# Two column vectors of a decoder layer: summed on the vector engine behind the head instead of on the tensor engine among the attention units

## The chip, the cores and the metric

One core of one Trainium2 chip. A kernel is timed in device microseconds from start to end of one launch; lower is better. Shown are the median, the lowest and the highest of three timed runs, and one further execution under the hardware profiler, whose trace is read here. The engines are TensorE (PE; its weight loads are PEld), VectorE (DVE), ScalarE (ACT), GpSimd (POOL) and SyncE (SP), which here issues nearly all DMAs. Each engine works through its own list of instructions in a fixed order.

## The reference, cut to what matters

One decoder layer on a sequence of 512 positions of width 1024, in float32. A conditioning vector c (1024) gives six vectors of 1024 by one matrix (1024 x 6144):

```python
mod = c @ w_ada[l] + b_ada[l]
sh1, sc1, gt1, sh2, sc2, gt2 = jnp.split(mod, 6, axis=-1)
h = rms_norm(x, g_pre_mix[l]) * (1.0 + sc1[:, None]) + sh1[:, None]
proj = h @ w_in[l]
...   # two attention groups: compressed/selected/window, and top-k sparse attention
x = x + gt1[:, None] * rms_norm(o, g_post_mix[l])
h = rms_norm(x, g_pre_ffn[l]) * (1.0 + sc2[:, None]) + sh2[:, None]
y = jnp.square(jax.nn.relu(h @ w_up[l])) @ w_down[l]
x = x + gt2[:, None] * rms_norm(y, g_post_ffn[l])
```

The change is about `sh2` and `sc2`, two of the six vectors: each a sum over 1024 rows of c times a row of 1024 numbers of `w_ada`, with a bias. They are needed when the second norm's output is made.

## The kernel before

Stages, in order of time: the head (0 to about 72 us: x is normed, transposed and multiplied with the first input weights, while sh1 and sc1 are summed); the projections (to about 145 us: chunks A, B, D, C, E of the input projection, rope, splitting of each float32 operand into a high and a low part, the indexer's scores); the attention units (to about 340 us: twelve units, with output projections between them); the second norm and the MLP (to the end). Products of split operands are three matmuls instead of one.

Order: steps are Python functions. `PLAN` (line 41) gives each group of steps a place t0 and a length dt; `place` (826) spreads the group's steps over numbered slots, and slot n is emitted with step n of the projection's pipeline (845 to 857, n from 0) or, from slot 19 on, with an attention unit (1083 to 1104). The framework then schedules all emitted instructions on a modelled time line: each engine's list is fixed before the run, and an instruction that comes later in the program can go ahead of one that is not ready in the model. `held` (592) makes a load come behind the loads of chunk D on SP's queue. `run` and `mix` (55 to 66) interleave lists evenly.

The six vectors: sh1 and sc1 in the head (`mod_sums`, 279). The gate gt1 is summed on TensorE by `vec_steps` (717) in group g1 = (17, 6). The gate gt2 is summed on DVE by `acc_steps` (672), with two loads and more ahead, beside the first MLP steps. The vectors sc2 (called a2) and sh2 go through `col_steps` (762), which uses `vec_steps`: eight loads of 512 KB each for a vector (two buffers with the tag vw, shared with gt1's loads), four matmuls for each load in four column groups of 32 (line 731), then for each half an ACT copy (767), four matmuls with a column of ones that turn the row into columns (770) and a DVE step with the bias (772). Groups a2 = (25, 2) and sh2 = (29, 3) put them among the attention units. Their results are used by `h2_steps` (1067, 1069).

Other names used: rw_C, rw_D, rw_E are raw weights of the chunks, uh and ul their high (ACT, 123) and low (DVE or POOL, 124) parts; pjB is B's projection, whose rope runs on POOL (`B1`, 478, and `rope`, 407); rwo_a and rwo_b are weights of the output projection; wk and m are the top-k rounds (574 to 579); mx is the row maximum of an attention unit (889). PSUM has four banks with the tag S, shared by projections, scores and these sums. The tag r (four buffers) is used from the MLP on (1141).

Of the kernel before, what the change touches and what calls it, by code (L numbers as in the profile page):

```python
# [9 lines left out]
F32 = mybir.dt.float32  # L10
# [3 lines left out]
OP = mybir.AluOpType  # L14
# [3 lines left out]
P = 128  # L18
T = 512
NT = 4  # L20
D = 1024
KT = 8
# [17 lines left out]

PLAN = dict(
    E=(19, 2.5), tk2=(17.8, 3.5), wa0=(25, 0.672), op00=(25.2, 0.48), wa1a=(25.1, 0.784), op10=(26.5, 0.462),
    wa1b=(25.73, 0.452), op01=(29.16, 0.2), op11=(27, 0.3), x20=(31.2, 0.1), x21=(27.3, 0.548), a2=(25, 2),
    sh2=(29, 3), wb0=(26.7, 0.49), wb1a=(28, 0.122), tk3=(21.5, 2.45), op20=(30.8, 0.48), wb1b=(30.5, 0.343),
    op21=(31.2, 0.96), op30=(32.5, 0.1), op31=(32.6, 0.49), h20=(32.2, 1.098), h21=(32.1, 0.549),
    x22=(32.6, 0.1), h22=(33.35, 1.68), x23=(33.6, 0.1), sD=(0, 0.48), cl=(0.2, 4.48), lC=(0.5, 0.1),
    sC=(3.7, 2.94), lE=(8.2, 0.1), sE=(8.3, 5.379), ix=(8.2, 5.88), cpe=(10, 0.1), ck1=(11.1, 1.077),
# [1 line left out]
    g1=(17, 6),  # L49
# [20 lines left out]
def layer_kernel(  # L70
# [7 lines left out]
    V, A, G, PE, SY = nc.vector, nc.scalar, nc.gpsimd, nc.tensor, nc.sync  # L78

    cst = ctx.enter_context(tc.tile_pool(name="cst", bufs=1))  # L80
    big = ctx.enter_context(tc.tile_pool(name="big", bufs=1))
# [23 lines left out]
    def m2(name, dt=F32):  # L105
        return big.tile([P, 512], dt, tag="m2", name=name, bufs=N_M)

    def st(shape, name):
        return sml.tile(shape, F32, tag="s%d" % int(np.prod(shape[1:])), name=name,
                        bufs=12 if shape[1] <= 8 else 2)  # L110

    def bank(tag, name, dt=F32):
        return psp.tile([P, 512], dt, tag=tag, name=name, bufs=4 if tag == "S" else 2)
# [16 lines left out]
    wa = w_ada[0].rearrange("(p k) n -> p k n", k=KT)  # L130
    wiv = w_in[0].rearrange("(k p) n -> p k n", p=P)
    xv = x[0].rearrange("(t p) d -> t p d", p=P)
    c_sb = cst.tile([P, KT], F32, name="c_sb")
# [48 lines left out]
    ones = cst.tile([P, P], F32, name="ones")  # L182
# [28 lines left out]
    colT = cst.tile([P, P], F32, name="colT")  # L211
# [122 lines left out]
    def behind(done, f, *args):  # L334

        with ExitStack() as es:
            for ins in done:
                es.enter_context(tc.issue_after(ins.ins))
            return f(*args)
# [203 lines left out]
    def Q2(nm, t):  # L543
        rv = heads(pjs[nm, t], 8)
        sks[nm, t] = [stack(rv[:, g * 4:g * 4 + 4, :], 4, f"{nm}{t}{g}", G) for g in range(2)]

    def Q3(nm, t):
        q = b4(f"q{nm}_{t}", F32R).rearrange("p (h q) -> p h q", q=P)
        for g in range(2):
            ps = stack_T(sks[nm, t][g], 4, f"{nm}{t}{g}")  # L550
            A.copy(q[:, g * 4:g * 4 + 4, :], ps.rearrange("p (h q) -> p h q", q=P))
        (qn if nm == "C" else qd)[t] = q
# [28 lines left out]
    def topk_steps(t):  # L581
        return [lambda: topk_round(t)] * 16 + [
            lambda: V.tensor_scalar(work[t], work[t], -3.2e38, NEG, op0=OP.is_gt, op1=OP.mult)]
# [8 lines left out]
    def held(f):  # L592

        return lambda: behind(d_loads[-1:], f)
# [122 lines left out]
    def vec_steps(c0, nm, finish):  # L717

        stt = {}

        def load(i):
            stt[i] = big.tile([P, 4, 256], F32, tag="vw", name=f"wv_{nm}{i}", bufs=2)
            n, q = divmod(i, 2)
            SY.dma_start(stt[i], wa[:, 4 * q:4 * q + 4, c0 + n * 256:c0 + n * 256 + 256])

        def mm(i):
            half, n, q = i // 4, i // 2 % 2, i % 2
            if i % 4 == 0:
                stt["ps"] = bank("S", f"vs_{nm}{half}")
            for j in range(4):  # L730
                PE.matmul(stt["ps"][32 * j:32 * j + 32, n * 256:n * 256 + 256],
                          c_sb[:, 4 * q + j:4 * q + j + 1].to_broadcast([P, 32]), stt[i][:, j, :],
                          start=(q == 0), stop=(q == 1))
            if i % 4 == 3:
                finish(half, stt["ps"])
        nv = 2
        seq = [lambda i=i: load(i) for i in range(nv)] + [none] * 6
        for i in range(8):
            seq.append(lambda i=i: mm(i))
            if i + nv < 8:  # L740
                seq.append(lambda i=i: load(i + nv))
        return seq
# [16 lines left out]
            V.tensor_tensor(g, pg, g, op=OP.mult)  # L759
        return [begin] + vec_steps(c0, "g1", finish)  # L760

    def col_steps(c0, nm):
        dst = cst.tile([P, KT], F32, name="col_" + nm)

        def finish(half, ps):
            acc = m2(f"acc_{nm}{half}")
            A.copy(acc, ps)
            pc = bank("S", f"cv_{nm}{half}")
            for k in range(4):
                PE.matmul(pc[:, k:k + 1], acc[:, k * P:(k + 1) * P], ones[:, 0:1], start=True, stop=True)  # L770
            h = half * 4
            V.scalar_tensor_tensor(dst[:, h:h + 4], pc[:, 0:4], 1.0 / 32.0,
                                   colT[:, c0 // P + h:c0 // P + h + 4], op0=OP.mult, op1=OP.add)
        return dst, vec_steps(c0, nm, finish)


    def w_in_chunk(c0, c1, nm, eng=V):
# [7 lines left out]
        def spl(i):  # L785
# [13 lines left out]
            lambda t, nm=nm: Q2(nm, t), lambda t, nm=nm: Q3(nm, t)), t) for t in range(NT) for nm in "C"]  # L799
    tl += tD + tC  # L800
    ix = [(t, h) for t in range(1, NT) for h in range(4)]
    tk = {t: topk_steps(t) for t in range(1, NT)}
    g1s = g1_steps(2 * D, g_post_mix)
    a2, a2s = col_steps(4 * D, "a2")
    sh2, sh2s = col_steps(3 * D, "sh2")
    a2s.append(lambda: V.scalar_tensor_tensor(a2, a2, 1.0, colT[:, 56:64], op0=OP.add, op1=OP.mult))
    el = []
    for t in range(NT + 2):
        if t < NT:
# [10 lines left out]
        ck1=[lambda: cmp_pack("k")], cv1=[lambda: cmp_pack("v")],  # L820
        ck2=[lambda: cmp_mm("k", 0), lambda: cmp_mm("k", 1)], cv2=[lambda: cmp_mm("v", 0), lambda: cmp_mm("v", 1)],
        ck3=[lambda: cmp_gelu("k"), lambda: cmp_out("k")], cv3=[lambda: cmp_gelu("v"), lambda: cmp_out("v")],
        tk1=tk[1], tk2=tk[2], tk3=tk[3], g1=[held(f) for f in g1s[:3]] + g1s[3:], a2=a2s, sh2=sh2s)
    slots = {n: [] for n in range(40)}

    def place(groups):
# [18 lines left out]
    for n in range(len(tl) + 3):  # L845
# [5 lines left out]
        while mm_done < min(want, len(mm_seq)):  # L851
            f, t = tl[mm_seq[mm_done]]
# [200 lines left out]
    def h2_steps(j):  # L1053
        def part(half):
# [8 lines left out]
            for i in range(4):  # L1063
# [14 lines left out]
               op11=outp_steps("a", 1, 1), x20=x2_steps(0), x21=x2_steps(1),  # L1078
               wb0=wout_steps("b", 0), wb1a=wb1[:2], op20=outp_steps("b", 2, 0), op30=outp_steps("b", 3, 0),
               wb1b=wb1[2:], op21=outp_steps("b", 2, 1), op31=outp_steps("b", 3, 1),  # L1080
               h20=h2_steps(0), h21=h2_steps(1), x22=x2_steps(2), x23=x2_steps(3), h22=h2_steps(2)))
    prev = None
    for n in range(16):
# [18 lines left out]
        if u is not None and u.nm == "w":  # L1102
            pc = cc
# [44 lines left out]
    def finish(t, half):  # L1148
        hs = [slice(i * 512, i * 512 + 512) for i in range(2)]
        jk = m2(f"fj_{t}{half}")  # L1150
        A.activation(jk, yacc[t][:, hs[half]], AF.Square, accum_out=sy[t][:, half:half + 1])
        (V if t == NT - 1 else G).tensor_tensor(yacc[t][:, hs[half]], yacc[t][:, hs[half]],
                                                res["g2"][:, hs[half]], op=OP.mult)
        if half == 1:
            rs = st([P, 1], "ro")
            rstd_of(rs, sy[t], V)
            for i in range(2):
                V.scalar_tensor_tensor(yacc[t][:, hs[i]], yacc[t][:, hs[i]], rs, x2[t][:, hs[i]],
                                         op0=OP.mult, op1=OP.add)
                SY.dma_start(ov[t][:, hs[i]], yacc[t][:, hs[i]])  # L1160
# [163 lines left out]
```

## Time and profile before

| | |
|---|---|
| timed runs | median 724.51 us (720.13 to 725.61) |
| profiled execution, own time | 724.97 us |
| its span, first to last instruction | 723.2 us |
| busy: PE / DVE / ACT / POOL | 674.7 / 510.3 / 373.9 / 191.9 us |
| mean granted clock of TensorE | 0.967 |

Busy times are of the whole span; stages differ, so the rows below are by stage. In a row of a timeline or a group stand line, engine, operation, output and inputs by the program's names (buffer numbers left out: vs_a2 is shown as vs_a), then shapes. In the chain of waits each piece is what released the next one, followed back from the last instruction.

### The profile page before, as it was taken

The numbers are of one execution on the slowest core, as the hardware profiler recorded it, in microseconds if no ns is written. First come the engines' busy times: TensorE is split into PE (matmuls) and PEld (weight loads), VectorE is DVE, ScalarE is ACT, GpSimd is POOL, SyncE is SP. The second block draws the span as 40 slices with busy tenths as digits, with TensorE's granted clock in tenths as the row PEclk, the third lists the DMA queues.
The fourth block names the chain that finished last, engine by engine and source line by source line (L and its number), as shares of the span: only waits on it lengthen the run. The fifth ranks groups of instructions, "written<-read, shape, count | busy, mean of one in ns | idle before, by whom it ended". The sixth has DMA issues, their size and how long they took to land.

```text
span 723.2 us, 10022 instructions
## 1 busy us (share of the span) xinstructions
PE 674.7 (93%) x3529; PEld 523.1 (72%) x3529; DVE 510.3 (71%) x1020; ACT 373.9 (52%) x755; POOL 191.9 (27%) x228
## 2 busy tenths in 40 slices
PE   3999989899998999799978999999999999999994
PEld 2678968777565676365668878888888888888883
DVE  5555458988997989775686539677597459695445
ACT  5343785435795669544464555433554355454221
POOL 3000285734523134222020022201140032231023
PEclk9899989999997999999999999999999999999998
DMA  9976630530316471462295212452144312322103
GB/s 293 311 232 188 199 88 1 117 116 30 118 30 191 133 171 30 117 233 87 65 339 156 90 54 85 145 178 57 29 146 146 116 30 58 88 88 93 53 1 116
DMA packets 91611, 87.15 MB, mean 121 GB/s; under 512 B 3909, under 2 KB 71593, under 8 KB 91562
## 3 DMA queue, kind: packets, MB, share of 16 engines
q1 hardware_dynamic: 91170, 86.46, 39.7%
q8 instruction: 28, 0.46, 0.3%
q14 instruction: 21, 0.17, 0.1%
q10 hardware_dynamic: 392, 0.06, 0.0%
HBM read 84.40 MB, written 2.10 MB: 120 GB/s over the span
## 4 chain that ended last, share of the span: by engine, by line
PE 74%; DVE 14%; DMA 4%; ACT 3%; POOL 2%; issue 2%; POOLq 0%; DVEq 0%; ACTq 0%; SPq 0%
PE up L1126 23%; PE dn L1254 15%; PE dn L1187 5%; PE op L1019 5%; PE pA L324 3%; PE O L918 3%; PE pB L324 2%; PE pj_E L324 2%; DVE wk L579 1%; PE pj_D L324 1%; DVE m L576 1%; DMA rwo_b<-in_w_out_dram 1%; DMA wg_g<-in_w_ada_dram 1%; PE tp_d L912 1%; PE pj_C L324 1%
## 5 line engine op out<-in xcount | busy, mean ns | idle before, releaser
L1126 PE MATMUL up<-hh,uh_U 128*128 128x512 f32 (+1 forms) x288 | 105.9, 369 | 3.2 <-ACT hh L123 2.7
L1126 PE MATMUL up<-hl,uh_U 128*128 128x512 f32 (+1 forms) x288 | 104.8, 369 | 1.0 <-DVE hl L124 1.0
L1126 PE MATMUL up<-hh,ul_U 128*128 128x512 f32 (+1 forms) x288 | 105.5, 368 | 0.0
L1216 POOL TENSOR_TENSOR r<-r,r 128x512 f32<-128x512 f32 x18 | 36.8, 2055 | 184.6 <-ACT r L1131 114.0
L123 ACT CAST th<-rd 128x1024 fp32r<-128x1024 f32 x42 | 44.2, 1053 | 75.1 <-PE dn L1254 40.6
L124 DVE TENSOR_TENSOR tl<-rd,th 128x1024 fp32r<-128x1024 f32 x42 | 53.9, 1288 | 39.4 <-ACT th L123 39.4
L124 DVE TENSOR_TENSOR ul_U<-rw_U,uh_U 128x1024 fp32r<-128x1024 f32 x32 | 43.1, 1346 | 32.8 <-ACT uh_U L123 32.6
L1126 PEld LDWEIGHTS up<-hh,uh_U 128*128 128x128 f32 x288 | 54.9, 191 | 12.7 <-ACT hh L123 3.2
L1126 PEld LDWEIGHTS up<-hl,uh_U 128*128 128x128 f32 x288 | 54.5, 191 | 10.0 <-DVE hl L124 1.2
L1126 PEld LDWEIGHTS up<-hh,ul_U 128*128 128x128 f32 x288 | 54.9, 191 | 8.7
L123 ACT CAST uh_U<-rw_U 128x1024 fp32r<-128x1024 f32 x32 | 33.6, 1049 | 50.9 <-PE up L1126 32.3
L1254 PE MATMUL dn<-th,sl 128*128 128x512 f32 x168 | 52.1, 391 | 0.3
L1254 PE MATMUL dn<-th,sh 128*128 128x512 f32 x168 | 51.9, 393 | 0.0
L1254 PE MATMUL dn<-tl,sh 128*128 128x512 f32 x168 | 51.7, 389 | 0.0
L1254 PEld LDWEIGHTS dn<-th,sh 128*128 128x128 f32 x168 | 31.5, 188 | 7.5 <-DVE usum L1241 0.6
L1254 PEld LDWEIGHTS dn<-th,sl 128*128 128x128 f32 x168 | 31.3, 188 | 7.6 <-DVE sl L124 1.2
L1254 PEld LDWEIGHTS dn<-tl,sh 128*128 128x128 f32 x168 | 31.5, 188 | 6.6
L1216 DVE TENSOR_TENSOR rd<-rd,rd 128x1024 f32<-128x1024 f32 x24 | 31.5, 1324 | 0.3
L123 ACT CAST sh<-r 128x512 fp32r<-128x512 f32 x42 | 25.2, 619 | 9.0 <-POOL r L1216 8.6
L124 DVE TENSOR_TENSOR sl<-r,sh 128x512 fp32r<-128x512 f32 x42 | 27.9, 710 | 0.0
L1241 DVE TENSOR_TENSOR y<-y,dn 128x512 f32<-128x512 f32 x40 | 25.5, 680 | 2.2 <-PE dn L1254 2.2
L576 DVE MAX8 m<-wk 128x8 f32<-128x256 f32 (+2 forms) x48 | 26.5, 552 | 0.7 <-POOL wk L571 0.4
(426 smaller groups left out, 1685.2 us busy)
## 6 DMA issues: line engine op xcount, KB each, us to landing
rw_U<-in_w_up_dram SPq DMA_DIRECT2D x32, 512.0 KB, 4.1
rd<-in_w_down_dram SPq DMA_DIRECT2D x24, 512.0 KB, 4.7
wm<-in_w_ada_dram SPq DMA_DIRECT2D x32, 256.0 KB, 6.1
x<-in_x_dram SPq DMA_DIRECT2D x8, 512.0 KB, 6.5
wv_g<-in_w_ada_dram SPq DMA_DIRECT2D x8, 512.0 KB, 6.9
rwo_a<-in_w_out_dram SPq DMA_DIRECT2D x16, 256.0 KB, 4.5
wv_a<-in_w_ada_dram SPq DMA_DIRECT2D x8, 512.0 KB, 4.0
rwo_b<-in_w_out_dram SPq DMA_DIRECT2D x16, 256.0 KB, 4.7
```

What stands on the lines that cost most here:

```text
L123: A.copy(hi, src)
L124: eng.tensor_tensor(lo, src, hi.bitcast(F32), op=OP.subtract)
L324: return PE.matmul(ps[:, :n], l[:, t, k, :], r[:, k % 2, :n], start=(k == 0 and i == 0), stop=(k == KT - 1 and i == 2))
L576: mx = V.max(m8, work[t])
L579: V.match_replace(work[t], m8, work[t], MARK)
L918: mm = [PE.matmul(O[j][g * 64:(g + 1) * 64, :], vn[kb][:, self.vsl[g]:self.vsl[g] + 64], pts[kb, g][0], start=(first and kb == 0), stop=(l ...
L1019: PE.matmul(stt["ps"], l[:, kk, :], r[:, kk % 2, :], start=(kk == 0 and i == 0), stop=(kk == 7 and i == 2))
L1126: PE.matmul(pv[:, t0:t1, :], l[:, k, :], r[:, t0:t1, k, :], start=(n == 0), stop=(n == 23))
L1187: PE.matmul(ps, l[:, t * P:(t + 1) * P], r[:, f % 2, :], start=(n == 0), stop=(n == 11))
L1216: eng.tensor_tensor(dst, x, y, op=op)
L1241: V.tensor_tensor(ya, ya, ps, op=op)
L1254: PE.matmul(ps[t], l[:, f, t * P:(t + 1) * P], r[:, f, :], start=(n == 0), stop=(n == 11))
```

## The change

`col_steps` takes both vectors and no longer uses `vec_steps`. It takes all four buffers of the tag r (two accumulators of 128 x 1024, two ring buffers) and both of the tag vw (two more ring buffers), makes 16 loads of whole rows (128 partitions x 1024 numbers, 512 KB each), adds each on DVE to the accumulator, scaled by c's column, and at the end of a vector makes eight matmuls with a column of ones on TensorE and one DVE step with the bias. The first four loads are held behind chunk D's loads; each further load follows the add that frees its buffer. The groups a2 and sh2 go from `PLAN`; c2 = (1, 9) is new. The factor 1/32 goes, since a sum is no longer held 32 times.

```diff
--- before.py
+++ after.py
@@ -40,8 +40,8 @@
 
 PLAN = dict(
     E=(19, 2.5), tk2=(17.8, 3.5), wa0=(25, 0.672), op00=(25.2, 0.48), wa1a=(25.1, 0.784), op10=(26.5, 0.462),
-    wa1b=(25.73, 0.452), op01=(29.16, 0.2), op11=(27, 0.3), x20=(31.2, 0.1), x21=(27.3, 0.548), a2=(25, 2),
-    sh2=(29, 3), wb0=(26.7, 0.49), wb1a=(28, 0.122), tk3=(21.5, 2.45), op20=(30.8, 0.48), wb1b=(30.5, 0.343),
+    wa1b=(25.73, 0.452), op01=(29.16, 0.2), op11=(27, 0.3), x20=(31.2, 0.1), x21=(27.3, 0.548),
+    c2=(1, 9), wb0=(26.7, 0.49), wb1a=(28, 0.122), tk3=(21.5, 2.45), op20=(30.8, 0.48), wb1b=(30.5, 0.343),
     op21=(31.2, 0.96), op30=(32.5, 0.1), op31=(32.6, 0.49), h20=(32.2, 1.098), h21=(32.1, 0.549),
     x22=(32.6, 0.1), h22=(33.35, 1.68), x23=(33.6, 0.1), sD=(0, 0.48), cl=(0.2, 4.48), lC=(0.5, 0.1),
     sC=(3.7, 2.94), lE=(8.2, 0.1), sE=(8.3, 5.379), ix=(8.2, 5.88), cpe=(10, 0.1), ck1=(11.1, 1.077),
@@ -759,19 +759,43 @@
             V.tensor_tensor(g, pg, g, op=OP.mult)
         return [begin] + vec_steps(c0, "g1", finish)
 
-    def col_steps(c0, nm):
-        dst = cst.tile([P, KT], F32, name="col_" + nm)
-
-        def finish(half, ps):
-            acc = m2(f"acc_{nm}{half}")
-            A.copy(acc, ps)
-            pc = bank("S", f"cv_{nm}{half}")
-            for k in range(4):
-                PE.matmul(pc[:, k:k + 1], acc[:, k * P:(k + 1) * P], ones[:, 0:1], start=True, stop=True)
-            h = half * 4
-            V.scalar_tensor_tensor(dst[:, h:h + 4], pc[:, 0:4], 1.0 / 32.0,
-                                   colT[:, c0 // P + h:c0 // P + h + 4], op0=OP.mult, op1=OP.add)
-        return dst, vec_steps(c0, nm, finish)
+    def col_steps(cols):
+
+
+        dsts, accs = [], []
+        for c0, nm in cols:
+            dsts.append(cst.tile([P, KT], F32, name="col_" + nm))
+            accs.append(big.tile([P, 2, 512], F32, tag="r", name="acc_" + nm, bufs=4).rearrange("p a n -> p (a n)"))
+        ring = [big.tile([P, 2, 512], F32, tag="r", name=f"wv_{i}", bufs=4).rearrange("p a n -> p (a n)")
+                for i in range(2)]
+        ring += [big.tile([P, 4, 256], F32, tag="vw", name=f"wv_{i + 2}", bufs=2).rearrange("p a n -> p (a n)")
+                 for i in range(2)]
+
+        def load(i):
+            SY.dma_start(ring[i % 4], wa[:, i % KT, cols[i // KT][0]:cols[i // KT][0] + D])
+
+        def add(i):
+            acc, k = accs[i // KT], i % KT
+            if k == 0:
+                V.tensor_scalar(acc, ring[i % 4], c_sb[:, 0:1], None, op0=OP.mult)
+            else:
+                V.scalar_tensor_tensor(acc, ring[i % 4], c_sb[:, k:k + 1], acc, op0=OP.mult, op1=OP.add)
+
+        def finish(v):
+            pc = bank("S", f"cv_{v}")
+            for k in range(KT):
+                PE.matmul(pc[:, k:k + 1], accs[v][:, k * P:(k + 1) * P], ones[:, 0:1], start=True, stop=True)
+            cb = cols[v][0] // P
+            V.tensor_tensor(dsts[v], pc[:, 0:KT], colT[:, cb:cb + KT], op=OP.add)
+        seq = [lambda i=i: load(i) for i in range(4)]
+        n = KT * len(cols)
+        for i in range(n):
+            seq.append(lambda i=i: add(i))
+            if i + 4 < n:
+                seq.append(lambda i=i: load(i + 4))
+            if i % KT == KT - 1:
+                seq.append(lambda i=i: finish(i // KT))
+        return dsts, seq
 
 
     def w_in_chunk(c0, c1, nm, eng=V):
@@ -801,9 +825,9 @@
     ix = [(t, h) for t in range(1, NT) for h in range(4)]
     tk = {t: topk_steps(t) for t in range(1, NT)}
     g1s = g1_steps(2 * D, g_post_mix)
-    a2, a2s = col_steps(4 * D, "a2")
-    sh2, sh2s = col_steps(3 * D, "sh2")
-    a2s.append(lambda: V.scalar_tensor_tensor(a2, a2, 1.0, colT[:, 56:64], op0=OP.add, op1=OP.mult))
+    (a2, sh2), c2s = col_steps([(4 * D, "a2"), (3 * D, "sh2")])
+    c2s = [held(f) for f in c2s[:4]] + c2s[4:]
+    c2s.append(lambda: V.scalar_tensor_tensor(a2, a2, 1.0, colT[:, 56:64], op0=OP.add, op1=OP.mult))
     el = []
     for t in range(NT + 2):
         if t < NT:
@@ -820,7 +844,7 @@
         ck1=[lambda: cmp_pack("k")], cv1=[lambda: cmp_pack("v")],
         ck2=[lambda: cmp_mm("k", 0), lambda: cmp_mm("k", 1)], cv2=[lambda: cmp_mm("v", 0), lambda: cmp_mm("v", 1)],
         ck3=[lambda: cmp_gelu("k"), lambda: cmp_out("k")], cv3=[lambda: cmp_gelu("v"), lambda: cmp_out("v")],
-        tk1=tk[1], tk2=tk[2], tk3=tk[3], g1=[held(f) for f in g1s[:3]] + g1s[3:], a2=a2s, sh2=sh2s)
+        tk1=tk[1], tk2=tk[2], tk3=tk[3], g1=[held(f) for f in g1s[:3]] + g1s[3:], c2=c2s)
     slots = {n: [] for n in range(40)}
 
     def place(groups):
```

## Rows read from the trace of the kernel before

**Rows 1.** The page's first line: the span, and the instructions in it

```profile
span 723.2 us, 10022 instructions
```

**Rows 2.** Busy by stage: length, PE, PEld, DVE, ACT, POOL, clock, DMA share, GB/s

```profile
61.00:72.00 11.00, 11.00 (x54) 9.49 (x53) 7.79 (x17) 4.31 (x9) 1.40 (x1) 1.00 0.90 270
72.00:84.00 12.00, 12.00 (x80) 11.06 (x78) 6.56 (x18) 8.18 (x22) 0.07 (x1) 1.00 1.00 308
84.00:99.00 15.00, 14.96 (x105) 13.52 (x103) 7.69 (x16) 13.74 (x37) 13.79 (x31) 1.00 0.35 99
99.00:104.00 5.00, 2.08 (x11) 1.61 (x12) 0.92 (x2) 4.81 (x14) 5.00 (x10) 0.76 0.07 25
104.00:112.00 8.00, 8.00 (x29) 6.35 (x28) 4.11 (x13) 2.98 (x10) 2.61 (x7) 0.72 0.01 3
112.00:150.00 38.00, 34.91 (x192) 29.76 (x191) 37.66 (x108) 20.77 (x53) 27.10 (x33) 0.96 0.24 56
223.00:262.00 39.00, 38.55 (x222) 23.44 (x223) 33.42 (x88) 22.62 (x48) 11.99 (x8) 0.87 0.65 182
300.00:320.00 20.00, 17.58 (x105) 9.68 (x106) 17.26 (x44) 14.95 (x35) 3.31 (x4) 0.91 0.67 213
320.00:361.00 41.00, 40.19 (x230) 25.16 (x229) 23.72 (x39) 16.67 (x35) 7.01 (x8) 1.00 0.26 78
```

**Rows 3.** Chain of waits by line: 205-300 (and one piece), 300-361

```profile
by line: PE op L1019 16.5%; DMA rwo_b<-in_w_out_dram 10.0%; PE O L918 9.4%; DVE P_d L907 6.6%; PE tp_d L912 6.5%; PE vs_a L731 3.8%; DVE uol_a L124 3.7%; DVE P_d L889 3.5%; PE O L969 2.8%; PE tp_s L912 2.8%; DVE wk L579 2.8%; DVE m L576 2.6
...
241.54 0.79 PE cv_a L770 x8
...
by line: PE op L1019 31.0%; PE O L918 18.0%; PE tp_w L912 6.5%; DMA wv_sh<-in_w_ada_dram 5.8%; PE vs_sh L731 4.8%; PE tp_d L912 4.1%; PE s_d L886 3.6%; PE tp_s L912 3.4%; PE cv_sh L770 2.9%; DVE x L1043 2.3%; PE s_d L887 2.3%; DVE uol_b L12
```

**Rows 4.** Groups of TensorE instructions, 205 to 361 (count, busy us, mean ns, idle)

```profile
L731 PE MATMUL vs_a<-wv_a,c_sb 128*32 128x256 f32 x64 | 5.1, 418 | 1.2 <-DVE mx L889 1.2
...
L731 PE MATMUL vs_sh<-wv_sh,c_sb 128*32 128x256 f32 x64 | 4.7, 388 | 0.2 <-DMA wv_sh<-in_w_ada_dram 0.2
```

**Rows 5.** Groups of DVE instructions, whole run: durations by form

```profile
L691 DVE SCALAR_TENSOR_TENSOR acc_g<-wg_g,c_sb,acc_g 128x512 f32<-128x512 f32 x16 | 11.8, 746 | 4.0 <-DMA wg_g<-in_w_ada_dram 4.0
...
L1026 DVE TENSOR_TENSOR on<-op,g 128x512 f32<-128x512 f32 x8 | 5.5, 683 | 0.0
...
L124 DVE TENSOR_TENSOR uol_a<-rwo_a,uoh_a 128x1024 fp32r<-128x1024 f32 x4 | 4.9, 1216 | 0.1
```

**Rows 6.** Timeline of POOL, then of DVE, near 90 to 96 (start us, us)

```profile
90.86 1.19 POOL L410 TENSOR_TENSOR ra_Bc<-pjB,rsin 128x64 f32<-128x64 f32 x1
92.01 0.32 POOL L412 TENSOR_TENSOR ra_Bc<-pjB,rsin 128x64 f32<-128x64 f32 x1
...
94.78 0.45 POOL L415 TENSOR_TENSOR pjB<-pjB,ra_Bc 128x128 f32<-128x128 f32 x1
95.20 1.44 POOL L415 TENSOR_TENSOR pjB<-pjB,ra_Bs 128x128 f32<-128x128 f32 x1
...
90.34 1.52 DVE L124 TENSOR_TENSOR ul_C<-rw_C,uh_C 128x1024 fp32r<-128x1024 f32 x1 [2.49 <-ACT uh_C L123]
...
95.08 1.24 DVE L124 TENSOR_TENSOR ul_C<-rw_C,uh_C 128x1024 fp32r<-128x1024 f32 x1 [0.58 <-ACT uh_C L123]
```

**Rows 7.** Chain of waits in 84 to 104, by line

```profile
by line: PE pj_D L324 18.1%; POOL pjB L415 15.7%; POOL pjB L414 11.4%; POOL ra_Bs L412 9.1%; POOL ra_Bc L410 8.9%; POOL ra_Bs L410 4.4%; POOL ra_Bc L412 4.2%; PE pj_C L324 4.0%; ACT k1s L432 3.7%; ACT k2s L433 3.7%; ACT kcp_k L622 3.6%; ACT
```

**Rows 8.** ACT's timeline at 74; waits of TensorE in 80 to 205

```profile
74.78 1.05 ACT L123 CAST uh_C<-rw_C 128x1024 fp32r<-128x1024 f32 x1 [6.14 <-DMA rw_C<-in_w_in_dram]
...
PE pj_E L324 <- DVE mx L889: 3.1, 1, 3.1
```

**Rows 9.** SP's queue at 63 to 67; first sums of the first norm's gate

```profile
63.50 0.98 SPq L724 DMA_DIRECT2D wv_g<-in_w_ada_dram  x2
66.67 3.08 SPq L783 DMA_DIRECT2D rw_C<-in_w_in_dram  x4
...
L731 PE MATMUL vs_g<-wv_g,c_sb x64: 379/390/486, 151.4 to 194.1; 128*32 128x256 f32 x64
```

## What is predicted, and how

> **What bounds the kernel now.** I read the page's span first [rows 1], then a table of busy time by stage [rows 2], then the chain of waits in the two stages that the edit touches [rows 3, 7], then single instructions for prices. The profiled execution took 724.97 us, 1.8 us of it outside its span [rows 1]; the median of the three timed runs is 724.51, 0.5 below that execution. The sum is made against the execution and its difference is laid on the median.
>
> In the table the reader is to see three different situations. From 61 to 99 us TensorE has no gap (11.0 of 11.0, 12.0 of 12.0, 14.96 of 15.0 us) while the DMA engines are full until 84 (share 0.90 and 1.00) [rows 2]. From 99 to 104 TensorE is busy only 2.1 of 5 us, and the chain of 84 to 104 tells why: POOL's rope for B's four tiles sets it, pjB 27.1% and the ra_Bc and ra_Bs pieces 26.6% of 20 us [rows 7]. From 112 to 150 DVE is full (37.7 of 38 us) [rows 2]. Among the attention units TensorE is the first limit (38.6 of 39 us in 223 to 262, 40.2 of 41 us in 320 to 361) and DVE the next (33.4 and 23.7) [rows 2].
>
> **What is taken away.** The two vectors' sums on TensorE are 64 records each, 5.1 and 4.7 us busy [rows 4]; four tiles side by side make each record cheap. On the chain they and what hangs on them are: vs_a 3.8% of the 95 us from 205 to 300, that is 3.6 us; cv_a 0.8; then, of the 61 us from 300 to 361, vs_sh 4.8% (2.9), cv_sh 2.9% (1.8) and the landing of a wv_sh load 5.8% (3.5) [rows 3]. Sum 12.6 us. All of it goes from this stretch, but DVE is late next, and its idle time caps the gain: 39 - 33.4 = 5.6 us for the 4.4 of 223 to 262 (passes); 20 - 17.3 = 2.7 us in 300 to 320, where the landing and some 1.8 us of vs_sh lie, 5.3 together (capped at 2.7); 41 - 23.7 = 17.3 for the remaining 2.9 (passes) [rows 2, 3]. I take 4.4 + 2.7 + 2.9 = 10.0 us. Upper bound: every record and column sum was on the path, 5.1 + 4.7 + 2 x 1.8 and the 3.5 of the landing, 16.9 [rows 3, 4]. Lower bound: in 205 to 300 the chain also passes the landing of rwo_b, 10.0% [rows 3]; if that holds the stage, its 4.4 are lost and 5.6 remain. The four ACT copies and small DVE steps that go were on neither path: nothing.
>
> **What is added, and what hides it.**
>
> *DVE work.* 16 instructions of 128x1024. None of this form is in the trace. The same operation on 128x512 takes 746 ns; a two-input subtraction takes 683 at 512 and 1216 at 1024, so I add the difference, 533: 1.28 us each, 20.5 us in all [rows 5]. (Bounds 1.22 and 1.49, the larger row alone and twice the small one.) DVE's idle time from 72 to 112 is 5.4 + 7.3 + 4.1 + 3.9 = 20.7 us [rows 2], so it is priced at nothing there; if the adds come after 112, where DVE is full, they cost their length.
>
> *Loads.* 16 of 512 KB, 8.4 MB. From 61 to 84 the queue moves 270 and 308 GB/s [rows 2], 289 in the mean: 1.8 us a load. What it carries there already is 6.7 MB; two wv_g loads of the first norm (1.05 MB) leave this place, because the new ring takes both vw buffers until its last adds; three rw_E loads (1.6 MB) follow [rows 9]. 6.7 - 1.05 + 1.6 + 8.4 = 15.6 MB, or 54 us: the last ring load lands near 115. So about two adds fall past 112. The top-k rounds that fill DVE there are due only for later units, so I let them move instead: cost 0, bound the ring's last four adds, 5.1 us. The wv_g loads that now wait behind the ring are first used at 151 us [rows 9], 36 us later: nothing.
>
> *The load of C.* The first rw_C load is issued behind the two wv_g loads [rows 9], and ACT already stands 6.1 us for it [rows 8], with A's and B's evacuations and casts queued behind it on ACT. Four ring loads instead of two put 2 x 1.8 = 3.6 us more ahead. ACT's idle time behind that wait is about 1.0 us to 84 (12 - 8.2, less the 2.8 us of the wait that lie after 72) and 1.3 us to 99 [rows 2]. 3.6 - 2.3 = 1.3 us pass to the chain; bounds 0 and 3.6. On SP, a reload that waits for the add which frees its buffer holds the rw_E loads behind it; only ACT's split of E waits for these, and POOL's and DVE's part of it behind ACT.
>
> *POOL.* POOL's rope steps lengthen when a long two-input DVE instruction runs beside them: 0.32 becomes 1.19 us under the one at 90.34, 0.45 becomes 1.44 under the one at 95.08 [rows 6], 0.93 us for each. From 84 to 99 some 8 loads land, 3 of them rw_E's, so 5 adds meet POOL where POOL is the chain [rows 7]: 5 x 0.93 = 4.7 us. Bounds: 0, if they fall into POOL's gaps; 7.4 with all 8.
> The Trainium skill, "SBUF — State Buffer", section "Who interferes with whom", says that such a DVE instruction and a POOL instruction that reads SBUF hold a shared port pair in turn for their whole length. By it each add would cost up to its own 1.28 us, the term would be 6.4 and the whole sum 1.7 us worse; the two lengthened rows stay under that because POOL came in after DVE had begun.
>
> *TensorE's column sums* come to 1.8 us a vector [rows 3]. The first falls into the gap at 99 to 104, the second before the 3.1 us that TensorE waits for DVE (pj_E behind mx) [rows 8]: 0; bound 3.6, if both covers go.
>
> **Sum.** -10.0 + 1.3 + 4.7 = -4.0 us: 724.97 becomes 721.0, and on the medians 724.51 becomes 720.5. Ends: -16.9 + 0, or 707.6; -5.6 + 5.1 + 3.6 + 7.4 + 3.6 = +14.1, or 738.6. A measurement of this kernel can tell about 1%, 7.2 us, from no change, so this is no change.
>
> **Rivals.**
> *All hidden (faster).* Adds land where POOL is idle and DVE too; then only the units speak: -10 to -16.9, 707.6 to 714.5. For it: POOL is busy 0.1 us of 72 to 84 and 2.6 of 104 to 112, and DVE has 20.7 idle us for 20.5 [rows 2]. Against it: by 84 only the first four loads or so can have landed.
> *DVE stands at late loads (slower).* DVE works in order, so an add written ahead of its load stops what is behind it: A's rope, C's splits, the ks stacks, hence POOL and TensorE. Adds need 1.28 us and loads 1.8, and the write order seems to hope for earlier loads than it gets: ACT stood 6.1 us for rw_C [rows 8], and DVE stood 4.0 us for wg_g in eight loads of the same kind of ring [rows 5]. If the adds are written to end near 99 and the loads end at 115, 16 us of waiting come in: -10 + 6.0 + 16 = +12, 736.5. It decides from 11.2 us of waiting on (-4.0 + 11.2 = 7.2). Against it: eight loads cost only 4.0 us.
> *The units don't get shorter.* DVE or the rwo_b loads take over at once: -5.6 + 6.0, 724.9, again no change.
>
> **How the numbers follow.** Chances: partly given back, 0.36 (715 to 730); units not shorter, 0.10; all hidden, 0.31; late loads, 0.23. Faster by over 1% (below 717.3) is the hidden case, 0.31; within 1% the first two, 0.46; slower (above 731.8) the late loads, 0.23. The range 709 to 736 cuts about one in ten off either side of the ends 707.6 and 738.6.
>
> **What would show it.** No TensorE record of the ada sums and no wv_sh landing among the units, and the stretch that began at 223 and ended at 361 some 10 us shorter: the gain. POOL's pjB rope ending more than 4 us after 99 with rows of 1 us and more beside adds: the loss. DVE rows idle before an add until a wv load, above 11 us in all: the slower rival. The prediction is wrong if POOL's rope ends where it did, or if the last add is far from 115.

## The result, and the profile after

The changed kernel takes 725.82 us in the median of 20 runs (723.33 to 728.36), the kernel before beside it 721.60 (717.70 to 725.61): ratio 1.0055, 95% interval 1.0037 to 1.0073. It is 4.0 us slower, where the forecast was 4.0 us faster; both lie within the 1% called no change, and the sign is wrong. The kernel before ran 2.9 us under the 724.51 that the forecast started from, so from here on differences are compared and not times.

The two profiled executions stand the other way round (spans 723.2 before [rows 1] and 722.7 after), so their ends say nothing. Stages can be compared: TensorE begins chunk B at 71.9 us before and at 71.4 after. By stage, columns as in [rows 2], the changed kernel:

```profile
61.00:72.00 11.00, 10.66 (x51) 8.82 (x50) 8.43 (x16) 4.69 (x10) 1.40 (x1) 1.00 1.03 368
72.00:84.00 12.00, 12.00 (x81) 11.14 (x80) 12.00 (x24) 7.61 (x20) 0.00 (x0) 1.00 1.05 385
84.00:99.00 15.00, 13.19 (x99) 12.01 (x97) 13.42 (x24) 13.13 (x35) 14.46 (x21) 1.00 1.02 345
99.00:104.00 5.00, 3.04 (x12) 2.67 (x13) 2.15 (x4) 0.70 (x3) 5.00 (x12) 0.66 0.86 289
104.00:112.00 8.00, 3.00 (x17) 2.13 (x15) 5.92 (x6) 6.38 (x19) 7.35 (x10) 0.92 0.02 8
112.00:150.00 38.00, 34.80 (x172) 30.08 (x173) 31.95 (x84) 17.68 (x41) 18.94 (x23) 0.84 0.26 70
...
300.00:320.00 20.00, 16.60 (x84) 9.53 (x83) 16.62 (x43) 13.88 (x33) 3.45 (x4) 1.00 0.45 110
320.00:361.00 41.00, 39.31 (x201) 25.80 (x200) 28.18 (x48) 18.95 (x39) 8.04 (x8) 1.00 0.41 141
```

Two things differ from [rows 2]. The queue moves 368, 385 and 345 GB/s where it moved 270, 308 and 99: the ring's loads are quick. And TensorE is busy 3.0 us of the 8 from 104 to 112, where it had no gap. Its timeline there (start us, us; in brackets the idle time before it and what ended it):

```profile
105.68 0.46 PE L426 MATMUL skp_ks<-identr,sk_ks 128*128 128x128 f32 x4
109.72 0.36 PE L426 MATMUL skp_ks<-identr,sk_ks 128*128 128x128 f32 x2 [3.57 <-DVE acc_sh L782]
110.87 0.50 PE L426 MATMUL skp_ks<-identr,sk_ks 128*128 128x128 f32 x2 [0.79 <-ACT k2s L434]
112.76 0.28 PE L611 MATMUL pep_k<-identr,perow 16*128 16x16 f32 x1 [1.40 <-ACT k2s L434]
113.91 0.28 PE L611 MATMUL pep_v<-identr,perow 16*128 16x16 f32 x1 [0.87 <-ACT k2s L434]
114.13 0.49 PE L426 MATMUL skp_kw<-identr,sk_kw 128*128 128x128 f32 x2
116.19 3.57 PE L787 MATMUL cv<-ones,acc_sh 128*128 128x1 f32 x16 [1.57 <-DVE acc_sh L782]
119.63 0.56 PE L561 MATMUL ix<-k1a,qi 128*128 128x256 f32 x1
119.99 0.41 PE L562 MATMUL ix<-k2a,qi 128*128 128x256 f32 x1
120.20 0.63 PE L324 MATMUL pj_C<-uh_C,hh 128*128 128x512 f32 x1
```

From 105.7 to 119.6 TensorE does only small transposes and the second vector's column sum (`cv`). Chunk C's second tile comes at 120.20; in the kernel before it is at

```profile
103.31 0.80 PE L324 MATMUL pj_C<-uh_C,hh 128*128 128x512 f32 x1 [2.14 <-ACT rl L564]
```

The wait of 3.57 us is put down to the add, which ended at 109.69; ACT's `k2s` before it ended at 109.66, so the trace doesn't show that the add alone held TensorE there. The wait before `cv` has no such neighbour: the last add ends at 116.1. DVE's last adds, which the column sum waits for, and POOL beside the last one:

```profile
111.71 1.27 DVE L782 SCALAR_TENSOR_TENSOR acc_sh<-wv,c_sb,acc_sh 128x1024 f32<-128x1024 f32 x1
...
114.33 1.81 DVE L782 SCALAR_TENSOR_TENSOR acc_sh<-wv,c_sb,acc_sh 128x1024 f32<-128x1024 f32 x1
...
113.80 3.46 POOL L625 TENSOR_TENSOR kcp_k<-kcp_k,peT 128x512 f32<-128x512 f32 x2 [2.29 <-DVE peT L613]
```

And all instructions on the ring (durations in ns, smallest, median, largest; first and last start in us):

```profile
L775 SPq DMA_DIRECT2D wv<-in_w_ada_dram x16: 328/374/3157, 59.2 to 100.6; - x16
L782 DVE SCALAR_TENSOR_TENSOR acc_a<-wv,c_sb,acc_a x7: 1272/1279/1283, 67.2 to 85.1; 128x1024 f32<-128x1024 f32 x7
L782 DVE SCALAR_TENSOR_TENSOR acc_sh<-wv,c_sb,acc_sh x7: 1273/1414/1814, 89.6 to 114.3; 128x1024 f32<-128x1024 f32 x7
L780 DVE TENSOR_SCALAR acc_a<-wv,c_sb x1: 754/754/754, 63.0 to 63.0; 128x1024 f32<-128x1024 f32 x1
...
its engine sat idle before it (us, times) until:
  DMA wv<-in_w_ada_dram: 0.5, 1
```

The first vector's adds take what was computed for them; those of the second, many of them beside POOL, take 1.27 to 1.81 us, with a median of 1.41. DVE waits for a load once, 0.5 us. The length of the head can be read from chunk E's last matmul: the kernel before, then the changed one:

```profile
L324 PE MATMUL pj_E<-uh_E,hl x32: 388/393/628, 131.3 to 178.8; 128*128 128x512 f32 x32
```
```profile
L324 PE MATMUL pj_E<-uh_E,hl x32: 388/393/632, 146.6 to 190.4; 128*128 128x512 f32 x32
```

From B's first matmul that is 178.8 - 71.9 = 106.9 us before and 190.4 - 71.4 = 119.0 after. The head became 12.1 us longer, and the units gave most of it back. Between these two matmuls TensorE was idle for 7.8 us before and for 14.8 after, at granted clocks of 0.94 and 0.90.

### The profile page after: what moved, and what is told of

It reads as the page before. It is cut to its first block, busy times and chain, and to the rows that moved or that the text cites. A ratio compares the mean times of both kernels' runs of the same rounds, so it can differ in the third digit from the quotient of the medians.

```text
span 722.7 us, 9798 instructions
## 1 busy us (share of the span) xinstructions
PE 665.3 (92%) x3401; PEld 520.8 (72%) x3401; DVE 533.8 (74%) x1034; ACT 371.1 (51%) x751; POOL 201.6 (28%) x228
## 4 chain that ended last, share of the span: by engine, by line
PE 64%; DVE 17%; DMA 6%; issue 4%; ACT 4%; POOL 3%; SPq 1%; DVEq 0%; POOLq 0%; ACTq 0%
PE up L1150 23%; PE dn L1278 15%; PE dn L1211 5%; PE op L1043 4%; PE pA L324 2%; DMA wg_g<-in_w_ada_dram 2%; PE O L942 2%; DVE wk L579 2%; PE pj_E L324 2%; DVE m L576 2%; PE pB L324 2%; PE mp L286 1%; DVE P_d L931 1%; PE tp_w L936 1%; DMA x<-in_x_dram 1%
## 5 line engine op out<-in xcount | busy, mean ns | idle before, releaser
L1150 PE MATMUL up<-hh,ul_U 128*128 128x512 f32 (+1 forms) x288 | 106.6, 371 | 0.0
L1150 PEld LDWEIGHTS up<-hl,uh_U 128*128 128x128 f32 x288 | 55.2, 194 | 11.2 <-DVE hl L124 2.5
```

The source lines that it names most:

```text
L1150: PE.matmul(pv[:, t0:t1, :], l[:, k, :], r[:, t0:t1, k, :], start=(n == 0), stop=(n == 23))
```

## The experiments

Each kernel ran beside runs of the kernel before; "us" is (ratio - 1) times its median there (721.0, 722.2, 720.5 and 720.8 in the four groups; 721.6 for the changed kernel). The changed kernel has 20 runs, e12 9, e1, e5, e8, e9 and e11 6 each, the others 12. "Head" is the time from B's first to E's last matmul in the one profiled execution; it varies with the written order and is a guide only.

| run | ratio (95% interval) | us | head |
|---|---|---|---|
| changed kernel | 1.0055 (1.0037, 1.0073) | +4.0 | 119.0 |
| e1 no sums | 0.9871 (0.9840, 0.9902) | -9.3 | 106.9 |
| e2 loads, adds of 8 columns | 0.9957 (0.9935, 0.9979) | -3.1 | 110.1 |
| e3 both column sums in slot 22 | 1.0024 (0.9997, 1.0051) | +1.7 | 115.9 |
| e4 a2 on DVE, sh2 on TensorE | 0.9979 (0.9957, 1.0002) | -1.5 | 106.5 |
| e5 both on DVE, in the units | 1.0112 (1.0072, 1.0152) | +8.1 | 108.6 |
| e6 one-input adds | 1.0014 (0.9990, 1.0038) | +1.0 | 123.1 |
| e7 adds, no loads | 0.9972 (0.9948, 0.9996) | -2.0 | 107.9 |
| e8 column sums, no loads, adds of 8 columns | 0.9826 (0.9792, 0.9860) | -12.6 | 109.6 |
| e9 a2 in the head, sh2 late on DVE | 0.9894 (0.9875, 0.9913) | -7.6 | 106.5 |
| e10 loads of an eighth | 1.0008 (0.9986, 1.0030) | +0.6 | 116.3 |
| e11 second column sum in slot 13 | 0.9910 (0.9882, 0.9937) | -6.5 | 109.8 |
| e12 sh2 on DVE, a2 on TensorE | 0.9947 (0.9923, 0.9971) | -3.8 | 106.6 |
| e13 column sums in another bank | 1.0027 (1.0008, 1.0047) | +1.9 | 118.1 |
| e14 both column sums in slot 13 | 1.0031 (1.0010, 1.0052) | +2.2 | 117.2 |

### What each side is worth: e1

```diff
-    a2, a2s = col_steps(4 * D, "a2")          # before: loads, 64 matmuls, column sum
+    a2, a2s = ...  [lambda: V.tensor_copy(dst, colT[:, h:h + 8])]
```

> The kernel before without the two sums: the 16 loads, the matmuls, the column sums and their ACT copies are left out, so a2 and sh2 hold the bias alone and the output is not the layer's. Nothing is added behind the head. This measures what the attention units can give back by itself. Theory (the units' gain was right, the price behind the head was too low): 10 to 17 us faster than before, 705 to 712 us. Rival (the units give back little, because DVE or the rwo_b loads take over at once): 0 to 6 us faster, 716 to 722 us.

Measured 712.26 us, -9.3, just outside the 705 to 712 named. The units' gain is there, nearly as computed (9.3 of 10). If the units give the changed kernel the same, the change costs the head 4.0 + 9.3 = 13.3 us, not 6.0.

### Loads, adds and column sums apart: e2, e8, e7, e10

```diff
-            acc, k = accs[i // KT], i % KT                # e2 and e8
+            acc, k = accs[i // KT][:, 0:8], i % KT
-            SY.dma_start(ring[i % 4], wa[:, i % KT, c0:c0 + D])       # e8 and e7
+            if i < 4: G.memset(ring[i], 0.5)
+            SY.dma_start(ring[i % 4][:, 0:128], wa[:, i % KT, c0:c0 + 128])   # e10, memset too
```

(e2 and e8 also set their accumulators to zero on POOL at the start, and e7 and e8 drop the hold behind chunk D's loads.)

> The changed kernel with each add cut from 1024 to 8 columns (the accumulators are zeroed on POOL first; the sums are wrong by what is left out): loads, ring, waits on SP and column sums stay, DVE's 20 us go. Theory (the adds hold up POOL and DVE and stand in front of the second column sum): most of the loss goes, 707 to 714 us, and the first matmul of chunk E starts within 3 us of the kernel before (130.8 us). Rival (the 8 MB of loads delay C's and E's weights): it stays near the changed kernel, 720 to 726 us, with E's first matmul near 146 us.

> No loads (the ring is filled once by POOL), adds cut to 8 of 1024 columns, and the two column sums of TensorE in their place: what is left of the change in the head is its written order and the 16 ones-column matmuls (the output is not the reference's). Theory A (the 6 us that stay with cut adds are the column sums and their place ahead of the indexer and chunk C): 716 to 719 us, E's first matmul 137 to 141. Theory B (the 6 us were the loads): 711 to 714 us, E's first matmul near 129 to 132.

> The changed kernel with all 16 adds and column sums, but the ring buffers are filled once by a POOL memset in place of the 16 loads (so the output is not the reference's). Theory A (the loads take nothing from the head, 345 to 385 GB/s leaves room): 723 to 727 us, E's first matmul past 143 us. Theory B (the loads cost the part of the head's 13 us that was left when the adds were cut, 6 us): 718 to 721 us, E's first matmul near 140.

> The changed kernel with all adds and column sums in place and the same 16 loads in the same queue, but each carries 128 of 1024 columns, 64 KB in place of 512 KB; the rest of each ring buffer is filled once by POOL (so the output is not the reference's). Theory A (the bytes of the loads cost nothing; DVE's adds and the written order do): 724 to 727 us, E's first matmul 72 us or more behind B's first. Theory B (the bytes matter, since the second vector's adds come late by them): 716 to 720 us, E's first matmul at most 66 us behind B's first (59 in the kernel before).

e8, with the column sums alone in their places, is 12.6 us faster than before: both theories named slower times, and the nearer is the one by which column sums cost nothing by themselves (711 to 714). The 16 matmuls show no cost when what they sum is ready: the second set ran at 100.0 to 101.7, in TensorE's gap. (It came out 3 us under e1, but the two intervals overlap.) With the loads back (e2) 9.5 of this are gone, though neither the loads nor the tiny adds are long; at 718.28 us e2 lies between its two ranges. In e2 an add of 8 columns shows what they do (POOL, DVE, and the second sum on TensorE):

```profile
100.12 2.41 POOL L124 TENSOR_TENSOR ul_E<-rw_E,uh_E 128x1024 fp32r<-128x1024 f32 x1
...
100.24 2.32 DVE L781 SCALAR_TENSOR_TENSOR acc_sh<-wv,c_sb,acc_sh 128x8 f32<-128x8 f32 x1
...
111.35 3.57 PE L786 MATMUL cv<-ones,acc_sh 128*128 128x1 f32 x16 [0.33 <-DVE acc_sh L781]
```

The add stands behind POOL's whole subtraction, DVE's wk behind the add, ACT's rl behind wk (2.4 us), and TensorE's skp_ks behind ACT (5.6 us); the last add starts at 110.33, and the column sum follows, with chunk C behind it (115.4). So even adds of no length keep the second column sum late, because the loads decide where the adds are written.

e7 did not separate what it was to: freed of the loads, the adds were written at 4.6 to 28.4 us, where TensorE waits for DVE in the first stage; B's first matmul came at 81.3, some 10 us later, and behind it the head had the old length. In e10 the bytes are gone and 3.4 us with them, with E's first matmul 68.9 us behind B's: between the two theories. Its adds began at 59.9 and ended at 104.6, and POOL's rope, with a weight split written inside it, ended at 111.1 (101.8 before, also with a split inside it; 104.2 in the changed kernel, without).

### One vector only: e4 and e12

```diff
-    (a2, sh2), c2s = col_steps([(4 * D, "a2"), (3 * D, "sh2")])
+    (a2,), c2s = col_steps([(4 * D, "a2")])     # e4: c2=(1, 4.5); e12: the other vector
+    sh2, sh2s = col_pe(3 * D, "sh2")            # the old form; e4: sh2=(29, 3), e12: a2=(25, 2)
```

> Half the change: a2 is summed on DVE behind the head as in the changed kernel (8 loads, 8 adds, one column sum), sh2 on TensorE among the units as before. In the trace of the changed kernel a2's adds end at 86.4 us, while POOL waits for other work until 84.5; sh2's end at 116.1, in POOL's busy stretch. Theory (only the later adds cost): half of the units' gain, 5 to 8 us, for 1 to 3 us behind the head: 715 to 719 us, faster than both kernels. Rival (each add costs the same wherever it stands): half the change is half the loss, 722 to 725 us.

> The one-vector run with the vectors exchanged: sh2 is summed on DVE behind the head, a2 stays on TensorE among the units. Theory A (the prediction's terms: a2's part in the units is worth 4.4 us, sh2's 5.6 with the landing of its load): 716 to 719 us, a little faster than the other one-vector run (719.1). Theory B (TensorE's records are worth the same wherever they stand): 718 to 721 us, no difference from it.

Both heads are as long as before (106.5, 106.6): the first eight adds, at 61 to 86 us, show no cost there (e9 below bounds it at 1.7 us). The 13.3 us belong nearly all to the second vector. In the units sh2 is worth 3.8 and a2 1.5, in the order that the prediction gave them (5.6 and 4.4), though their intervals touch; the two add up to 5.3 of the 9.3, so a vector that stays on TensorE keeps more than its share; how was not followed up.

### The second column sum: e11

```diff
-            if i % KT == KT - 1:
-                seq.append(lambda i=i: finish(i // KT))
+            if i == KT - 1:
+                seq.append(lambda: finish(0))        # finish(1) goes to slot 13: c2f=(13, 0.2)
```

> The changed kernel with only the second vector's column sum and its two small DVE steps moved from slot 10 to slot 13, behind chunk C's tiles in the program. Theory A (what TensorE loses between 105 and 120 us is that chunk C's last three tiles and the indexer stand behind that column sum in its order, hence behind the last add): 715 to 720 us, E's first matmul at most 66 us behind B's first. Theory B (DVE's adds and POOL's rope cost it in any order): 723 to 727 us, E's first 70 us or more behind B's first.

713.99 us, -6.5, faster than either theory named: 10.5 us come back for one step moved (8 to 13 by the two intervals). With one step less to spread, three loads and one add also move one slot later, but the written order of all five engines is the changed kernel's up to the first skp_ks at 105.4. Then, at the same time as the idle stretch above:

```profile
105.44 0.46 PE L426 MATMUL skp_ks<-identr,sk_ks 128*128 128x128 f32 x4
105.73 0.35 PE L561 MATMUL ix<-k1a,qi 128*128 128x256 f32 x1
105.92 0.28 PE L562 MATMUL ix<-k2a,qi 128*128 128x256 f32 x1
108.22 0.50 PE L324 MATMUL pj_C<-uh_C,hh 128*128 128x512 f32 x1 [2.02 <-ACT pjC L537]
```

```profile
L782 DVE SCALAR_TENSOR_TENSOR acc_sh<-wv,c_sb,acc_sh x7: 1272/1341/1544, 89.2 to 114.9; 128x1024 f32<-128x1024 f32 x7
...
L787 PE MATMUL cv<-ones,acc_sh x16: 239/250/250, 130.6 to 132.3; 128*128 128x1 f32 x16
```

The last add still starts at 114.9, and POOL's rope still ends late (last kcT at 104.2). Only the indexer and chunk C no longer stand behind them, and from B's first to E's last matmul TensorE is idle for 7.8 us again, as in the kernel before. The mark set for E's first matmul (66 us behind B's) was missed, 73.8: E now begins behind hid_v, but ends at 180.7, 10 us earlier than in the changed kernel. The place of a first matmul was the wrong mark; its last one is the better.

### Why it stands there, and what else moves: e13, e3, e14

```diff
-            pc = bank("S", f"cv_{v}")         # e13
+            pc = bank("O", f"cv_{v}")
-    c2=(1, 9),                                # e3: c2f=(22, 2), e14: c2f=(13, 0.6), both sums there
+    c2=(1, 9), c2f=(13, 0.6),
```

> The changed kernel with one word altered: both column sums write a PSUM bank of the tag O, which the attention outputs use later, instead of one of the four banks of the tag S, which the indexer's scores and the chunk's projections share; adds, loads and the places of all steps stay. Theory A (a bank of S, handed out to the second column sum in program order and held until the last add has come, is what puts the indexer and chunk C's last three tiles behind it): the chunk's 24-matmul blocks no longer follow the column sum on TensorE, and the time is 713 to 719 us. Theory B (it is the place of the step, not the bank; or another loss appears in the head as soon as the order moves): 721 to 727 us.

> The changed kernel with one edit: the column sums on TensorE and what follows them go from behind the adds to slots 22 and 23, among the attention units. Adds and loads stay. Theory (TensorE's order puts the second column sum, which waits for the last add, ahead of the indexer and chunk C: 1.6 us of waiting, 3.6 at half clock, and what is queued behind): 4 to 8 us faster than the changed kernel, 718 to 722 us; E's first matmul near 138 to 141 us. Rival (POOL and DVE alone set that stretch, the column sums only fill a gap): within 2 us of the changed kernel.

> The changed kernel with both column sums moved to slot 13, where the run with only the second one moved gained 10 us, and the run with both moved to slot 22 gained 3. Theory A (slot 22 was too late, among the indexer's top-k rounds and E; the first sum's place does not matter): 712 to 717 us. Theory B (the first column sum has to stay in front: without it the planned order of POOL's and TensorE's steps in 84 to 104 us changes, POOL's rope for B ends past 110 as in the run with both in slot 22): 720 to 725 us.

In e13 the blocks of chunk C run from 110.7 on, and the second sum (122.6 to 124.2) stands inside the third of them, with nothing altered but the sums' bank: so the bank of the shared tag S, or the order planned around it, had held them back. The time did not follow: 1.9 us slower than before. Chunk C's last matmul starts 61.0 us behind B's first, where it is 68.4 in the changed kernel and 56.4 in e11, but E's last is only 0.9 us earlier than in the changed kernel: most of what chunk C wins is lost behind it. The written order ahead changed as well; by stage:

```profile
84.00:99.00 15.00, 11.43 (x94) 10.85 (x92) 11.62 (x20) 11.16 (x28) 14.16 (x24) 0.94 0.97 332
99.00:104.00 5.00, 5.00 (x14) 3.94 (x13) 5.00 (x7) 3.40 (x11) 5.00 (x7) 0.50 0.70 205
```

TensorE stands idle for 3.6 us of 84 to 99, and its granted clock then is 0.50 (the lower of its two levels, 1.2 GHz) over the five us from 99 to 104. In the changed kernel these are 1.8 us and 0.66, and its idle time over 84 to 104 is the same (3.8 us, e13 3.6), so little of e13's loss can lie here. e3 and e14 do lose in this stretch: TensorE is idle for 8.3 us from 84 to 104 in both. The longest wait of TensorE from 84 to 135 in e14, the same in e3 (us in total, times, longest):

```profile
PE kcT L495 <- POOL pjB L415: 8.3, 2, 5.0
```

Without the first column sum in its old place, chunk C's first block is written behind the third kcT, which waits 5.0 us for POOL's rope: it starts at 100.0 in e14 and 102.0 in e3, 94.7 in the changed kernel. So the theory that slot 22 was too late fell. That 84 to 104 is reordered holds, though its mark was wrong: the rope ended at 105.0 and 107.1, not past 110. That the first sum's removal does it isn't shown, since five loads and four adds move one slot later with it. And this stretch isn't most of the loss: chunk C's last matmul starts 57.9 us (e14) and 58.0 us (e3) behind B's first, only 1.5 later than in e11, while E's last is 7.4 and 6.1 later. So in e13, e3 and e14 alike most of the loss against e11 lies behind chunk C; what causes it, and why the planned order falls out so, no run here isolates.

### The form of the add, and other places: e6, e5, e9

```diff
-                V.scalar_tensor_tensor(acc, ring[i % 4], c_sb[:, k:k + 1], acc, op0=OP.mult, op1=OP.add)
+                V.tensor_scalar(acc, ring[i % 4], c_sb[:, k:k + 1], c_sb[:, k:k + 1], ...)    # e6
-    c2=(1, 9),
+    c2=(27, 5),                                                                  # e5
+    c2=(1, 4.5), sh2=(30.85, 1.2),      # e9; sh2's loads queued behind the last rwo_b load
```

> The changed kernel with its 14 two-input adds replaced by a one-input multiply-and-add of the same size, place and operands but without the running sum as second input (the accumulation is left out, so the output is not the reference's). Theory A (DVE's two-input form and POOL stand in each other's way): POOL's rope for B ends within 1.5 us of 99 as in the run with cut adds, POOL's rows lose their 1.3 us, and the time is 717 to 721 us, although DVE still works some 15 us on it. Theory B (what costs is DVE's own time, in whatever form): POOL's rope still ends past 102 and the time stays at 723 to 727 us.

> The changed kernel with its loads, adds and column sums moved whole from the slots behind the head to the slots 27 to 32 of the attention units (about 262 to 361 us). Theory A (the head's loss is a matter of place; DVE has room late in the units): DVE idles 2.7 us in 300 to 320 and 17.3 us in 320 to 361 of the kernel before, 20.0 for adds of 20.5, and TensorE still has its records back; E's first matmul comes within 2 us of the kernel before (130.8), and the time is 712 to 717 us. Theory B (adds in a place where DVE is nearly full cost their length, and POOL's and DVE's unit steps wait): the slots 27 to 29 lie in 262 to 300, where DVE is busy 36 of 38 us, so about half the adds, 10 us, are paid: 719 to 724 us, with E's first matmul just as early.

> The first vector stays on DVE behind the head as in the one-vector run; the second vector's loads are queued behind the last load of rwo_b (283 to 290 us) and its adds follow on DVE after them, some 290 to 335 us, where the kernel before leaves DVE idle 20 us of 61; no ada sum is left on TensorE. Theory A (a sum on DVE is free where DVE idles, and only the crowded stretches of 84 to 120 us and 196 to 250 us made it dear): the units' 9.3 us are gained, the head loses at most 2, 8 adds of 1.28 us partly show: 713 to 717 us. Theory B (whatever waits there for DVE is itself on the path, near the second norm): 719 to 724 us.

e6's time, 724.52 us, lies in the range of the theory that the hold on POOL isn't what costs. The one-input add takes 0.80 us in place of 1.28, and POOL's 0.32 us steps beside it 0.77 in place of 1.30:

```profile
96.65 0.77 POOL L412 TENSOR_TENSOR ra_Bs<-pjB,rsin 128x64 f32<-128x64 f32 x1
```

The second column sum still stands ahead of chunk C (122.2, chunk C at 126.1). Less DVE work and less hold on POOL, 3.0 us faster than the changed kernel: neither is the main cause.

e5 is the dearest, 730.51 us, slower than either theory named. The head is free, but the steps were written as soon as their buffers allowed, not where the slots stand:

```profile
L775 SPq DMA_DIRECT2D wv<-in_w_ada_dram x16: 327/330/1377, 64.1 to 230.2; - x16
L782 DVE SCALAR_TENSOR_TENSOR acc_a<-wv,c_sb,acc_a x7: 1272/1279/3403, 76.3 to 216.5; 128x1024 f32<-128x1024 f32 x7
L782 DVE SCALAR_TENSOR_TENSOR acc_sh<-wv,c_sb,acc_sh x7: 1255/1274/2485, 215.0 to 245.0; 128x1024 f32<-128x1024 f32 x7
```

Nearly all adds fall between 196 and 250, where DVE is the bound (66.7 of 73 us in 150 to 223, 36.9 of 39 in 223 to 262). Against e1 they cost 8.1 + 9.3 = 17.4 us, of some 20 us of adds. e9 holds the second vector's loads back until DVE has room:

```profile
L782 DVE SCALAR_TENSOR_TENSOR acc_sh<-wv,c_sb,acc_sh x7: 1253/1273/1279, 292.6 to 313.9; 128x1024 f32<-128x1024 f32 x7
```

713.11 us: 7.6 us under the kernel before, 1.7 short of e1. It beats both kernels, as e11 does, and lies in the range that its order was costed at (713 to 717).

## Why the prediction was wrong, step by step

**The units' gain** was right in size: 10.0 computed, 9.3 measured (e1).

**The loads** were mis-sized. The prediction took 289 GB/s, the old mix, and put the last landing near 115. With rows of 4 KB in one piece among its loads the queue moved 345 to 385 GB/s; the last load was issued at 100.6 and the queue fell silent at 104. So its 1.3 us for rw_C are 0 (ACT's uh_C starts at 74.58 without a wait for the load; 74.78 before, [rows 8]; ACT's own order had changed too, with B's copies written ahead of it). That the last add did come at 114.3 was right for a wrong reason: not its load was late, but its place in DVE's written order.

**DVE stands at late loads**, the slower rival, is false: 0.5 us of waiting, where 11.2 were needed. That the kernel became slower does not speak for it. The other two rivals fell as well: the units did get shorter, and the adds were not all hidden.

**POOL** was right as a mechanism and in size. Four adds each lengthen one step of its rope for B by 1.0 to 1.1 us (five adds at 0.93 were computed). Three of these steps, with two of the adds:

```profile
89.65 1.41 DVE L782 SCALAR_TENSOR_TENSOR acc_sh<-wv,c_sb,acc_sh 128x1024 f32<-128x1024 f32 x1
...
89.94 1.30 POOL L412 TENSOR_TENSOR ra_Bc<-pjB,rsin 128x64 f32<-128x64 f32 x1
...
96.41 1.30 POOL L412 TENSOR_TENSOR ra_Bs<-pjB,rsin 128x64 f32<-128x64 f32 x1
...
99.06 1.54 DVE L782 SCALAR_TENSOR_TENSOR acc_sh<-wv,c_sb,acc_sh 128x1024 f32<-128x1024 f32 x1
...
99.48 1.43 POOL L415 TENSOR_TENSOR pjB<-pjB,ra_Bc 128x128 f32<-128x128 f32 x1
...
103.28 0.46 POOL L415 TENSOR_TENSOR pjB<-pjB,ra_Bc 128x128 f32<-128x128 f32 x1
```

The last of these rows writes what the last kcT reads. It ends at 103.74; in the kernel before it ended at 99.06, and kcT followed:

```profile
99.12 0.33 PE L495 MATMUL kcT<-identr,pjB 128*128 128x128 f32 x1 [0.16 <-POOL pjB L415]
```

That is 4.7 us later, as computed. (The whole rope ends only 2.4 later, since E's split now stands behind it and not inside it.) But e11 keeps that late rope and all adds, and comes out 2.8 us behind e1, with intervals that overlap. The delay was charged to the end one for one; e11 shows that all of it together costs a few us at most, and can't say how many.

**DVE's adds** took 1.28 us in the first vector, as computed, and 1.41 in the median of the second. The last two began at 111.7 and 114.3, at a cost taken as nothing; together with POOL's delay and the loads they stay within e11's 2.8, as far as that is resolved.

**TensorE's column sums: 0** is the step that failed. They were costed by their own length, 1.8 us, the first was laid in the gap from 99 to 104 and the second before the 3.1 us in which pj_E waits for DVE [rows 8]; they ran at 87.0 and 116.2. What counts is what the instruction waits for and what is written behind it: the last add at 114.3 to 116.1, and the indexer and three blocks of 24 matmuls of chunk C, which the kernel before began at 103.3. That is 10.5 us (e11 against the changed kernel), TensorE's idle time in the head falls from 14.8 to 7.8 us with it, and with e11's 2.8 it makes the 13.3 of the head. What the wait by itself costs stays open: e13, e14 and e3 free chunk C as well, and keep most of the loss behind it. The prediction asked for DVE, SP and POOL what is queued behind a new wait, and didn't ask it for TensorE, the engine that bounds the stage. No rival named it.

The Trainium skill, "SBUF — State Buffer", section "Who interferes with whom", says that a DVE instruction with two SBUF inputs contends with a POOL instruction that reads SBUF, and that whichever issues first has the shared ports for its whole instruction. The rows agree in both directions: POOL's 0.32 us steps took 1.30 and 1.44 beside adds, and an add of 8 columns took 2.32 beside POOL's 2.41. The prediction weighed the first direction only.

## What to carry to other kernels

Work moved to an idle engine still ends in one instruction on the busy one; ask what that instruction waits for, and what is written behind it there, before asking how long it is. Moved work should be held until its engine has room: the same sums cost 17.4 us in the units' crowded part, and 1.7 with the first in the head and the second held back to 290 us. When a step is moved in a kernel whose order is planned, compare the written order of the bounding engine first: moving one step of eight short matmuls (16 records) was worth 10.5 us here.

## What the runs showed of the hardware

- With 16 loads of 128 rows of 4 KB among the others the queue moved 345 to 385 GB/s from 61 to 99 us, where the mix before reached 270, 308 and 99 [rows 2].
- The wait between DVE and POOL goes the other way too. DVE's wk (128x256, one tensor input; 0.40 us in the changed kernel) took 2.43 us beside POOL's subtraction of 2.41 (e6), and an add of 1.28 took 3.40 beside another such of 2.37 (e5).
- The first add of a vector, one input and one scalar, takes 0.75 us for 128x1024; with a second scalar 0.80; with a second tensor 1.28. POOL's steps of 0.32 us took 0.77 beside the 0.80 (e6) and 1.30 beside the 1.28.
- A column sum of 16 records took 1.9 us at a granted clock of 1.00 (the first, 87.0 to 88.9) and 3.57 at 0.50 (the second): TensorE had been busy 2.3 us of the 10.5 before it. The granted clock was 0.50 from 112 to 124, and chunk C's block began at 0.63 us a matmul, where others take 0.39. The kernel before began this block at 0.63 as well (103.9 to 108.2), so this is not a difference between the two.
